# Sixteen more tokens of an expert layer go row by row (144 instead of 128), and the orders around them move with it

## The chip, the cores and the metric

The kernel runs on one core of one Trainium2 chip. The metric is the device time of one execution in microseconds (us). Within one execution times are counted from the start of the profiled span. The engines are TensorE (PE; PEld is its loading of weights), VectorE (DVE), ScalarE (ACT), GpSimd (POOL) and SyncE (SP), which issues most DMAs.

## What is computed

Two transformer blocks over 512 tokens of width 1024 in float32. The change concerns the last layer of the second, a mixture of 16384 one-neuron experts. Each of 8 heads picks 16 experts per token out of 128 x 128 by two top-16 searches; the 128 picked experts of a token have a gate `g_c` each:

```python
    def chunk(args):
        h_c, e_c, g_c = args
        a = jnp.einsum('cd,ced->ce', h_c.astype(jnp.float32), u[e_c].astype(jnp.float32))
        act = jax.nn.gelu(a, approximate=False) * g_c
        return jnp.einsum('ce,ced->cd', act, v[e_c].astype(jnp.float32))
```

`u` and `v` are 16384 x 1024 matrices; the result is added to the residual `x`.

## The kernel before

**Two ways for the tokens.** The first `ND` = 384 tokens go densely: all 16384 experts are computed for them with matmuls, and a gate matrix with zeros for the experts that were not picked selects. The last 128 tokens go row by row: for each of their 128 picks, GpSimd gathers one row of `u` per token (128 rows of 4 KB, one token per partition), VectorE multiplies it with the token's `h` and sums (a dot product); later the same with `v`, where VectorE adds the scaled row to `rows_o`. That makes 128 u jobs and 128 v jobs, in this order, each one gather (`gather`, L1697) and one VectorE pass (`one_by_one`).

**Dense u stage.** 128 blocks of 128 experts. A block's weights (512 KB) are loaded by SP, ScalarE rounds them to a high part `wh` (L85), VectorE subtracts to get the low part `wl` (helper line L217), and TensorE runs 24 matmuls of `ND` columns: 8 slices of the contraction times hi x hi, hi x lo, lo x hi (L429 to L431). Four raw weight buffers and three of parts are in flight. For the first `NPRE` = 60 blocks the low part was made during the feed-forward stage and stored in DRAM (`made`); GpSimd's queue fetches it (L108). ScalarE applies Gelu (L1880), and SP writes the block's activations to DRAM (`a_d`).

**Gates.** Within the u stage, after the top-16 searches (`select`, on VectorE), `gates` makes the dense gate matrix in batches of 8 tokens: VectorE builds one-hot matrices, ScalarE scales one (L1810), TensorE multiplies them (16 f16 matmuls a batch, L1770), and ScalarE evicts four tokens at a time from PSUM into a tile `stg` laid out expert by token (L1774). Each full tile of `NG` = 48 tokens is written to DRAM (`g_d`, `put`).

**Dense v stage.** The 128 blocks of v in their order: eight blocks of activations and gates are fetched from DRAM at a time (`fetch`, tile `ag`, which shares its two buffers with `stg`), VectorE multiplies them, ScalarE and VectorE split the product into high and low parts two blocks at a time (`activate`), and 24 matmuls of `ND` columns (L1939 to L1941) add to eight PSUM banks. At the end the rows are transposed into the remaining 128 columns of the banks, VectorE adds the residual (L1948), and the result is stored.

**What sets the order.** The program is one stream for every engine, written by a host-side loop. TensorE's matmuls are its clock: after each slice of a block (8 slices) `later.tick()` advances the waiting generators, which put the work of the other engines in between; `yield n` means n ticks. `Balance` keeps a rough count of TensorE, VectorE and DMA work: `room(slack)` lets a generator wait while VectorE is more than `slack` columns behind TensorE, and `fill` (called in each tick) starts a row job when VectorE and the DMA count have room, up to `RATE` jobs per u block, and in the v stage evenly up to block 124. `LAG` is the number of ticks between the two halves of a split. Row buffers: `NUB` = 4 of one kind (`ub`), which before hold the scores of two heads, scratch of `select` (`small`) and the norm weights (`grow`).

Of the kernel before, what the change touches and what calls it, by code (L numbers as in the profile page):

```python
# [236 lines left out]
def tile_kernel(ctx, tc, a, out):  # L237
# [61 lines left out]
    ents([("v", j) for j in range(128)])  # L299
# [1216 lines left out]
    stream.LAG = 4  # L1516
# [11 lines left out]
    def row_buffer():  # L1528
        return c3.tile([128, D], F32, name="ub", bufs=NUB)

    scs = [row_buffer().rearrange("p (i t) -> p i t", i=2) for h in HEADS[:2]]
# [52 lines left out]
    def together(gens):  # L1584
# [22 lines left out]
    def select(t0, nt, places):  # L1607
# [5 lines left out]
        for h in HEADS:  # L1613
            while not {2 * h, 2 * h + 1} <= ready3:
# [4 lines left out]
            yield from together(  # L1619
                top16(scs[h][:, i, 128 * t:128 * t + 128], v[:, i, t - t0, :], ix[:, i, t - t0, :])  # L1620
                for i in range(2) for t in range(t0, t0 + nt))
            dv.tensor_copy(ixf, ix)
            cand, ixr, oneh = places(nt)
            yield from room()
# [3 lines left out]
            for i in range(2):  # L1628
# [3 lines left out]
            yield from together(  # L1632
                top16(cand[:, t].rearrange("p a b -> p (a b)"), gf[:, t0 + t, h, :], si[:, t, :])
                for t in range(nt))
# [5 lines left out]
            yield from room()  # L1640
            dv.tensor_tensor(oneh, sab.rearrange("p i t k -> p (i t) k")[:, :, None, :].to_broadcast(
                [128, 2 * nt, 16, 16]), iota16[:, None].to_broadcast([128, 2 * nt, 16, 16]), op=OP.is_equal)
            yield from room()
            for i in range(2):
                part = oneh[:, nt * i:nt * i + nt]
                dv.tensor_tensor(part, part, ixr[i], op=OP.mult)
                yield from room()
            for n in (8, 4, 2):
                dv.tensor_tensor(oneh[:, :, :n], oneh[:, :, :n], oneh[:, :, n:2 * n], op=OP.add)
                yield from room()  # L1650
# [3 lines left out]
            yield from room()  # L1654
# [10 lines left out]
        yield from room()  # L1665
        dv.reciprocal(z, z)
        yield from room()
        dv.tensor_tensor(g, g, z[:, :, :, None].to_broadcast(full), op=OP.mult)
        yield from room()
# [17 lines left out]
    dots = c3.tile([128, 128], F32, name="dots")  # L1687
    rows_h = c3.tile([128, KD, 128], F32, name="rows_h")
    flat = {"u": a["u_rows"], "v": a["v"].rearrange("b p d -> (b p) d")}
    jobs = [(what, s) for what in "uv" for s in range(128)]  # L1690
    got, stage = {}, {"at": 0}

    def gather(n):
        if n < len(jobs):
            what, s = jobs[n]
            got[n] = row_buffer()
            nc.gpsimd.indirect_dma_start(out=got[n], out_offset=None, in_=flat[what],  # L1697
                                         in_offset=bass.IndirectOffsetOnAxis(ap=idx[:, s:s + 1], axis=0))
            bal.transfer(D)

    def rows_in():
# [3 lines left out]
        for i in range(2):  # L1705
            pt = pst.tile([128, 512], F32, name="pt")
            for k in range(4):
                nc.tensor.transpose(pt[:, 128 * k:128 * k + 128], xT[:, 4 * i + k, ND:], identf)
# [8 lines left out]
        while not {(t, HEADS[i]) for t in (0, ND // 128) for i in range(2)} <= read:  # L1717
            yield 1
        for n in range(NUB):
            gather(n)  # L1720
        yield 20
        stage["go"] = stage.get("blk", 0)

    def one_by_one():
        n = stage["at"]
        if "go" not in stage or n == len(jobs):
            return
        what, s = jobs[n]
        if what == "v" and "out" not in stage:
            return  # L1730
        t = got.pop(n).rearrange("p (k f) -> p k f", k=8)
        if what == "u":
            dv.tensor_tensor_reduce(t, t, rows_h, 1.0, 0.0, OP.mult, OP.add, dots[:, s:s + 1])
            if s == 127:
                nc.scalar.activation(dots, dots, AF.Gelu)
        elif s == 0:
            dv.tensor_tensor(dots, dots, gf[:, 3].rearrange("p h k -> p (h k)"), op=OP.mult)
            dv.tensor_scalar(stage["out"], t, dots[:, s:s + 1], None, op0=OP.mult)
# [17 lines left out]
    def gates():  # L1756
# [5 lines left out]
        prev = stg = None  # L1762

        def products(oh2, og, b):
            for q in range(TG // 4):
                pg = pss.tile([128, 512], F32, name="ps")
                for i in range(4):
                    for r in range(2):
# [4 lines left out]
                k0 = (TG * b + 4 * q) % NG  # L1773
                nc.scalar.activation(stg[:, :, k0:k0 + 4].rearrange("p e t -> p t e"),  # L1774
                                     pg.rearrange("p (t e) -> p t e", t=4), AF.Copy, scale=1.0 / GS)
                yield 1

        for b in range(ND // TG):
# [25 lines left out]
            yield from room()  # L1804
            dv.tensor_tensor(oh1, ib, of(eb[:, 0, tk]), op=OP.is_equal)
            yield from room()
            dv.tensor_tensor(og[:, 0], oh1, of(gp[:, tk]), op=OP.mult)
            yield from room()
# [5 lines left out]
            if prev:  # L1814
                yield from products(*prev)
                if TG * b % NG == 0:
                    later.spawn(put(TG * b // NG - 1, stg))
            if TG * b % NG == 0:
                stg = c3.tile([128, 128, NG], F32, name="stg", bufs=2)
            prev = oh2, og, b  # L1820
        yield from products(*prev)
        later.spawn(put(ND // NG - 1, stg))

    def put(i, stg):
# [14 lines left out]
    def fetch(c):  # L1839

        if c < 16:
            t = c3.tile([128, 2, 8, ND], F32, name="ag", tag="stg", bufs=2)
            for i in range(2):
                nc.sync.dma_start(t[:, 0, 4 * i:4 * i + 4].rearrange("p b t -> p (b t)"),
                                  a_d[2 * c + i].rearrange("p b t -> p (b t)"))
                bal.transfer(4 * ND)
                yield P["f1"]
            for i in range(2):
                nc.sync.dma_start(t[:, 1, 4 * i:4 * i + 4], g_d[4 * i:4 * i + 4, :, 8 * c:8 * c + 8, :].rearrange(
                    "s p b t -> p s (b t)"))  # L1850
# [223 lines left out]
```

## Time and profile before

| | |
|---|---|
| median of 3 runs | 2462.03 us (2460.21 to 2464.12) |
| the profiled execution | 2467.27 us, span 2463.4 us |
| granted TensorE clock, mean | 0.993 |
| TensorE matmuls, busy | 2384.7 us (97%) |
| VectorE, busy | 1797.7 us (73%) |
| ScalarE, busy | 1219.2 us (49%) |
| GpSimd, busy | 477.8 us (19%) |
| moved by DMA | 643.37 MB, mean 261 GB/s |

Busy time is the union of an engine's instructions; matmuls are pipelined and overlap, so a TensorE that is busy all the time need not run at its best. The granted clock is told as a share of full speed. The DMA share is the mean busy share of 16 DMA engines and can pass 1.

### The profile page before, as it was taken

To read this page: it belongs to the slowest core of one execution; us is meant where nothing else is said; L and a number is where in the kernel's file an instruction comes from. 1 tells how busy PE (TensorE), PEld (TensorE's weight loads), DVE (VectorE), ACT (ScalarE), POOL (GpSimd) and SP (SyncE) were. 2 spreads that over 40 slices of the span, in tenths; PEclk is the share of its full clock that TensorE was granted. 3 is DMA by queue.
4 is the path that set the end of the run, shared out by engine and by line. 5 is a ranking of instruction groups with operands and counts; after the bars stand their busy time and mean duration, and the time that the engine had idled before them with its cause. 6 is when DMAs were issued, how large, how long until landed. Compare 5 with 4: busy or idle time off the path is not lost.

```text
span 2463.4 us, 36419 instructions
## 1 busy us (share of the span) xinstructions
PE 2384.7 (97%) x13139; PEld 2134.6 (87%) x13139; DVE 1797.7 (73%) x3587; ACT 1219.2 (49%) x2185; POOL 477.8 (19%) x538
## 2 busy tenths in 40 slices
PE   6899999999999999999999999999999999999998
PEld 5677778888777888777889999999999999999998
DVE  6678676555676777655688997787766888888886
ACT  3466444443545555533445344999973333333332
POOL 0310001000012100000001233322113433334331
PEclk9999999999999999999999999999999999999999
DMA  7873679898856543134326999999989999999994
GB/s 277 204 205 103 226 236 315 282 292 280 265 156 176 150 126 110 58 107 145 105 85 231 321 407 406 364 322 328 330 323 395 378 373 368 358 370 366 374 376 154
DMA packets 210580, 643.37 MB, mean 261 GB/s; under 512 B 25488, under 2 KB 62096, under 8 KB 210016
## 3 DMA queue, kind: packets, MB, share of 16 engines
q1 hardware_dynamic: 141360, 412.46, 47.7%
q0 software_dynamic: 68320, 227.97, 28.0%
q8 instruction: 103, 1.69, 0.3%
q14 instruction: 77, 0.63, 0.1%
q10 hardware_dynamic: 720, 0.62, 0.1%
HBM read 540.92 MB, written 100.17 MB: 260 GB/s over the span
## 4 chain that ended last, share of the span: by engine, by line
PE 80%; ACT 7%; DVE 5%; issue 4%; DMA 4%; POOL 1%; ACTq 0%; SPq 0%; DVEq 0%; POOLq 0%
PE pg L429 17%; PE pg L431 16%; PE pg L430 16%; PE pv L1939 7%; PE pv L1941 7%; PE pv L1940 7%; ACT ogh L1810 2%; ACT stg L1774 2%; ACT wh L85 1%; PE pt L654 1%; PE po L676 1%; DMA wl<-made 1%; PE ps L780 1%; PE ps L1770 1%; DMA ks<-bounce 1%
## 5 line engine op out<-in xcount | busy, mean ns | idle before, releaser
L429 PE MATMUL pg<-hh,wh 128*128 128x512 f32 (+1 forms) x2088 | 789.4, 378 | 5.9 <-ACT c_rcnt L968 1.7
L431 PE MATMUL pg<-hh,wl 128*128 128x512 f32 (+1 forms) x2088 | 763.7, 366 | 4.7 <-DMA wl<-made 4.1
L430 PE MATMUL pg<-hl,wh 128*128 128x512 f32 (+1 forms) x2088 | 763.0, 365 | 2.2 <-DVE hl L500 1.1
L85 ACT ACTIVATE wh<-wr 128x1024 fp32r<-128x1024 f32 (+2 forms) x446 | 466.4, 1046 | 406.1 <-PE pv L1940 189.1
L431 PEld LDWEIGHTS pg<-hh,wl 128*128 128x128 f32 x2088 | 394.6, 189 | 52.0 <-DMA wl<-made 6.3
L429 PEld LDWEIGHTS pg<-hh,wh 128*128 128x128 f32 x2088 | 395.1, 189 | 44.7 <-ACT wh L85 2.1
L430 PEld LDWEIGHTS pg<-hl,wh 128*128 128x128 f32 x2088 | 396.0, 190 | 36.5 <-DVE hl L557 2.0
L217 DVE TENSOR_TENSOR wl<-wr,wh 128x1024 fp32r<-128x1024 f32 x210 | 256.9, 1223 | 139.1 <-ACT wh L85 138.3
L88 DVE TENSOR_TENSOR wl<-wr,wh 128x1024 fp32r<-128x1024 f32 (+2 forms) x176 | 209.4, 1191 | 45.6 <-ACT wh L85 45.6
L1697 POOL DMA_INDIRECT ub<-in_v,idx x128 | 163.4, 1276 | 293.4 <-DVE rows_o L217 275.3
L1697 POOL DMA_INDIRECT ub<-in_u_rows,idx x128 | 157.2, 1228 | 310.3 <-DVE dots L217 292.4
L1939 PE MATMUL pv<-part,wh 128*128 128x384 f32 x512 | 172.0, 336 | 0.6 <-ACT full L1880 0.6
L1941 PE MATMUL pv<-part,wl 128*128 128x384 f32 x512 | 172.1, 336 | 0.0
L1940 PE MATMUL pv<-part,wh 128*128 128x384 f32 x512 | 171.9, 336 | 0.0
L1939 PE MATMUL pv<-parts,wh 128*128 128x384 f32 x512 | 171.5, 335 | 0.0
L1940 PE MATMUL pv<-parts,wh 128*128 128x384 f32 x512 | 171.4, 335 | 0.0
L1941 PE MATMUL pv<-parts,wl 128*128 128x384 f32 x512 | 171.2, 334 | 0.0
L217 DVE CUSTOM_DVE_ANT_0 ub<-ub,rows_h 128x1024 f32<-128x1024 f32 x128 | 155.1, 1218 | 16.4 <-DMA ub<-in_u_rows,idx 14.5
L217 DVE SCALAR_TENSOR_TENSOR rows_o<-ub,dots,rows_o 128x1024 f32<-128x1024 f32 x127 | 162.6, 1280 | 0.8
L1810 ACT ACTIVATE ogh<-oh,gT 128x128 f16<-128x128 f16 x384 | 120.5, 457 | 2.3 <-DVE oh L217 2.3
L95 DVE TENSOR_TENSOR pl<-wr,ph 128x1024 fp32r<-128x1024 f32 x60 | 73.3, 1222 | 52.1 <-ACT ph L93 50.6
L1880 ACT ACTIVATE full<-pg 128x384 f32<-128x384 f32 x86 | 44.6, 519 | 125.8 <-issue 102.8
(409 smaller groups left out, 4018.3 us busy)
## 6 DMA issues: line engine op xcount, KB each, us to landing
wr<-in_u SPq DMA_DIRECT2D x188, 512.0 KB
wr<-in_v SPq DMA_DIRECT2D x128, 512.0 KB
wr<-in_w_in SPq DMA_DIRECT2D x66, 512.0 KB
made<-pl POOLq DMA_DIRECT2D x60, 512.0 KB
wl<-made POOLq DMA_DIRECT2D x60, 512.0 KB
g_d<-stg SPq DMA_DIRECT2D x32, 768.0 KB
ag<-a_d SPq DMA_DIRECT2D x32, 768.0 KB
ag<-g_d SPq DMA_DIRECT2D x32, 768.0 KB
```

Source lines behind the costliest of these rows:

```text
L85: self.nc.scalar.activation(hi[:, :n], t[:, :n], AF.Copy)
L88: self.low.tensor_tensor(lo[:, :n], t[:, :n], hi[:, :n].bitcast(F32), op=OP.subtract)
L95: self.low.tensor_tensor(lo, t, hi.bitcast(F32), op=OP.subtract)
L217: return f(*args, **kw)
L429: nc.tensor.matmul(ps[:m, :n], w[0][:, wk], rh, start=first, stop=False)
L430: nc.tensor.matmul(ps[:m, :n], w[0][:, wk], rl, start=False, stop=False)
L431: nc.tensor.matmul(ps[:m, :n], w[1][:, wk], rh, start=False, stop=last)
L1697: nc.gpsimd.indirect_dma_start(out=got[n], out_offset=None, in_=flat[what], in_offset=bass.IndirectOffsetOnAxis(ap=idx[:, s:s + 1], axis=0))
L1810: nc.scalar.activation(og[:, 1, n // 2, :, n % 2], oh1[:, n // 2, :, n % 2], AF.Copy, scale=gT[:, tk.start + n:tk.start + n + 1])
L1939: nc.tensor.matmul(ps, wh[:, c], hi, start=b == 0, stop=False)
L1940: nc.tensor.matmul(ps, wh[:, c], lo, start=False, stop=False)
L1941: nc.tensor.matmul(ps, wl[:, c], hi, start=False, stop=b == 127)
```

## The change

16 more tokens (368 to 383) go row by row: `ND` is 368, and a second kind of job is added. For them a gather takes 8 picks of 16 tokens at once (partition 16 g + t), so 128 picks need `NE` = 16 u jobs ("x") and 16 v jobs ("y"). Their `h` rows are copied to eight groups of partitions by seven small DMAs, indices and gates are spread by 24 small DMAs (`extra_in`), and at the end a matmul with `fold` (eight identity matrices on top of each other, 16 columns) sums the groups. Gate tiles hold `NG` = 46 tokens, and the eviction's inner loop runs over four tokens instead of 128 experts. The v stage begins with blocks 120 to 127, whose activations ScalarE writes straight into `ag`, without `a_d`. Row buffers are two of kind `ub` and two of kind `uc` (the scores of two heads): the first two gathers go out when the row tokens' search is done, the others in `deeper`. The diff, cut:

```diff
+ORDER_V = [*range(120, 128), *range(120)]
-ND = 384
-NG = 48
-NUB = 4
-NPRE = 60
-RATE = 0.95
+ND = 368
+NS = 384
+NE = NS - ND
+NG = ND // 8
+NPRE = 58
+RATE = 1.06
...
-    stream.LAG = 4
+    stream.LAG = 5
...
-    def row_buffer():
-        return c3.tile([128, D], F32, name="ub", bufs=NUB)
-
+    def row_buffer(tag="ub"):
+        return c3.tile([128, D], F32, name="ub", tag=tag, bufs=2)
+    scs = [row_buffer("uc").rearrange("p (i t) -> p i t", i=2) for h in HEADS[:2]]
...
-    jobs = [(what, s) for what in "uv" for s in range(128)]
+    jobs = [(what, s) for pair in ("ux", "vy") for what, n in zip(pair, (128, NE)) for s in range(n)]
...
+    def deeper():
+
+        while not {(0, h) for h in HEADS[:2]} <= read:
+            yield 1
+        stage["deep"] = stage["next"]
+        for n in range(2):
+            gather(stage["next"])
...
-        while not {(t, HEADS[i]) for t in (0, ND // 128) for i in range(2)} <= read:
+        for n in range(2):
+            gather(n)
+        later.spawn(deeper())
+        while "u" in busy:
             yield 1
-        for n in range(NUB):
-            gather(n)
-        yield 20
+        stage["rows_x"] = rows_x = cst.tile([128, KD, 128], F32, name="rows_x", tag="silc")
+        for i in range(2):
+            pt = pst.tile([128, 512], F32, name="pt")
+            for k in range(4):
+                nc.tensor.transpose(pt[:NE, 128 * k:128 * k + 128], xT[:, 4 * i + k, ND:NS], identf)
+            yield 3
+            dv.tensor_tensor(rows_x[:NE, 4 * i:4 * i + 4, :], pt[:NE].rearrange("p (k f) -> p k f", k=4),
+                             grow[:NE, 512 * i:512 * i + 512].rearrange("p (k f) -> p k f", k=4), op=OP.mult)
+            yield 1
+        for g in range(1, 128 // NE):
+            nc.sync.dma_start(rows_x[NE * g:NE * g + NE], rows_x[:NE])
+        yield 10
         stage["go"] = stage.get("blk", 0)
+
+    def extra_in():
+
+
+        dv.scalar_tensor_tensor(idx_t, e1f[:, 2].rearrange("p h k -> p (h k)"), 128.0,
+                                e2f[:, 2].rearrange("p h k -> p (h k)"), op0=OP.mult, op1=OP.add)
+        yield 4
+        t = slice(ND % 128, 128)
+        for g in range(128 // NE):
+            p, c = slice(NE * g, NE * g + NE), slice(NE * g, NE * g + NE)
+            nc.sync.dma_start(idx_x[p], idx_t[t, c])
+            nc.sync.dma_start(gf_x[p], gf[t, 2].rearrange("p h k -> p (h k)")[:, c])
+            nc.sync.dma_start(rt_x[p], rt[t, 0, 2:3])
+            yield 2
+        yield 10
+        stage["more"] = True
 
...
-        if "go" not in stage or n == len(jobs):
+        if "go" not in stage or n == len(jobs) or (stage["next"] >= 128 and "more" not in stage):
...
+        own = what in "uv"
+        d = dots if own else dots_x
+        if what in "ux":
+            dv.tensor_tensor_reduce(t, t, rows_h if own else stage["rows_x"], 1.0, 0.0, OP.mult, OP.add, d[:, s:s + 1])
+            if s == d.shape[1] - 1:
+                nc.scalar.activation(d, d, AF.Gelu, scale=1.0 if own else rt_x)
         else:
-            dv.scalar_tensor_tensor(stage["out"], t, dots[:, s:s + 1], stage["out"], op0=OP.mult, op1=OP.add)
-        gather(n + NUB)
+            o = stage["out"][:, 0 if own else 1]
+            if s == 0:
+                dv.tensor_tensor(d, d, gf[:, 3].rearrange("p h k -> p (h k)") if own else gf_x, op=OP.mult)
+                dv.tensor_scalar(o, t, d[:, s:s + 1], None, op0=OP.mult)
+            else:
+                dv.scalar_tensor_tensor(o, t, d[:, s:s + 1], o, op0=OP.mult, op1=OP.add)
+        gather(stage["next"])
...
-                k0 = (TG * b + 4 * q) % NG
-                nc.scalar.activation(stg[:, :, k0:k0 + 4].rearrange("p e t -> p t e"),
-                                     pg.rearrange("p (t e) -> p t e", t=4), AF.Copy, scale=1.0 / GS)
+                t0 = TG * b + 4 * q
+                for i in range(t0 // NG, (t0 + 3) // NG + 1):
+                    if i not in stg:
+                        stg[i] = c3.tile([128, 128, NG], F32, name="stg", bufs=2)
+                    lo, hi = max(t0, NG * i), min(t0 + 4, NG * i + NG)
+                    nc.scalar.activation(stg[i][:, :, lo - NG * i:hi - NG * i],
+                                         pg.rearrange("p (t e) -> p e t", t=4)[:, :, lo - t0:hi - t0], AF.Copy,
+                                         scale=1.0 / GS)
+                    if hi == NG * i + NG:
+                        later.spawn(put(i, stg.pop(i)))
...
-            yield from room()
+            yield from room(3500)
...
+        yield 10
         if i == ND // NG - 1:
-            yield P["f0"]
-            yield from fetch(0)
-            later.spawn(activate(0), 2)
+            while 15 not in AG:
+                yield 1
+            yield from fetch_g(15)
+            while stage["blk"] < 123:
+                yield 1
+            later.spawn(activate(0), 8)
             yield from fetch(1)
 
...
+    def fetch(i):
+
+        if i < 16:
+            c = ORDER_V[8 * i] // 8
+            yield from fetch_a(c)
+            yield from fetch_g(c)
...
+            if b >= 120:
+                nc.scalar.activation((AG[15] if b > 120 else eight(15))[:, 0, b % 8], ps, AF.Gelu)
+                return
...
-    later.spawn(chain(select(3, 1, places1), rows_in()))
-    later.spawn(chain(select(0, 3, places3), gates()))
+    later.spawn(chain(select(3, 1, places1, 4500), rows_in()))
+
+    def spread_out():
+        later.spawn(extra_in())
+        yield 0
+
+    later.spawn(chain(select(0, 3, places3, 2000), spread_out(), gates()))
...
-    rows_o = hp.tile([128, 4, KD, 128], F32, name="rows_o", tag="hh")[:, 0]
+    rows_o = hp.tile([128, 4, KD, 128], F32, name="rows_o", tag="hh")[:, :2]
-    for b in range(128):
-        stage["blk"] = b
...
+    for g in range(1, 128 // NE):
+        nc.vector.tensor_tensor(fold, identf[:, :NE] if g == 1 else fold, identf[:, NE * g:NE * g + NE], op=OP.add)
     for d in reversed(range(8)):
-        nc.tensor.transpose(acc_o[d][:, ND:], rows_o[:, d, :], identf)
+        nc.tensor.transpose(acc_o[d][:, NS:], rows_o[:, 0, d, :], identf)
+        nc.tensor.matmul(acc_o[d][:, ND:NS], rows_o[:, 1, d, :], fold, start=True, stop=True)
         nc.vector.tensor_tensor(xT[:, d, :], acc_o[d], xT[:, d, :], op=OP.add)
```

`places3`, `top16`, `together` and `select` change only in taking a `slack`; `together` and `select` hand it to `room`. The v blocks' weights are streamed in `ORDER_V` too.

## Rows read from the trace of the kernel before

**Rows 1.** Busy by stretch: us, PE, PEld, DVE, ACT, POOL, clock, DMA share, GB/s.

```profile
1321.50:1921.40 599.90, 590.34 (x3823) 569.93 (x3821) 466.02 (x1180) 404.41 (x802) 166.88 (x171) 0.99 0.96 352
1410.00:1550.00 140.00, 140.00 (x803) 138.28 (x802) 112.22 (x427) 61.13 (x103) 51.35 (x62) 1.00 1.06 405
1556.00:1824.00 268.00, 262.90 (x1953) 245.40 (x1952) 210.40 (x299) 263.16 (x569) 64.10 (x56) 0.99 0.92 327
1921.40:2425.00 503.60, 503.60 (x2902) 503.60 (x2903) 424.23 (x407) 173.52 (x183) 184.59 (x142) 1.00 0.97 366
1921.40:2455.00 533.60, 533.60 (x3076) 533.57 (x3077) 437.05 (x419) 180.29 (x190) 184.59 (x142) 1.00 0.93 347
2200.00:2250.00 50.00, 50.00 (x290) 50.00 (x289) 41.51 (x38) 17.15 (x18) 17.31 (x14) 1.00 0.95 348
```

**Rows 2.** TensorE in order of time: start us, duration us, instruction; first and last.

```profile
1212.56 0.27 PE L1573 MATMUL ps<-kl,hi 128*128 128x128 f32 x1
...
1213.34 0.27 PE L1574 MATMUL ps<-kh,lo 128*128 128x128 f32 x1
...
499.66 0.39 PE L431 MATMUL pg<-hh,wl 128*128 128x512 f32 x1
...
501.25 0.39 PE L429 MATMUL pg<-hh,wh 128*128 128x512 f32 x1
...
1999.77 0.33 PE L1940 MATMUL pv<-parts,wh 128*128 128x384 f32 x1
...
2001.33 0.33 PE L1940 MATMUL pv<-parts,wh 128*128 128x384 f32 x1
```

**Rows 3.** Groups by line, 1300 to 2464: count, busy us, mean ns, idle before.

```profile
L85 ACT ACTIVATE wh<-wr 128x1024 fp32r<-128x1024 f32 x256 | 271.7, 1062 | 339.9 <-PE pv L1940 189.1 <-issue 147.4 <-PE pv L1941 3.4
L217 DVE TENSOR_TENSOR wl<-wr,wh 128x1024 fp32r<-128x1024 f32 x196 | 239.9, 1224 | 138.9 <-ACT wh L85 138.0 <-issue 0.6
...
L1774 ACT ACTIVATE stg<-ps 128x512 f32<-128x512 f32 x96 | 98.2, 1135 | 0.1
...
L1565 ACT ACTIVATE hi<-pg 128x512 fp32r<-128x512 f32 x2 | 1.2, 598 | 3.5 <-PE pg L431 3.5
```

**Rows 4.** Line L1774: count, shortest, median, longest ns, first and last start.

```profile
L1774 ACT ACTIVATE stg<-ps x96: 1055/1136/1258, 1556.6 to 1823.3; 128x512 f32<-128x512 f32 x96
```

**Rows 5.** Groups by line of TensorE, 1560 to 1826.

```profile
L429 PE MATMUL pg<-hh,wh 128*128 128x384 f32 x391 | 140.3, 359 | 0.0
...
L1770 PE MATMUL ps<-ogh,oh2h 128*128 128x128 f16 x752 | 60.8, 221 | 4.7 <-ACT stg L1774 2.4 <-ACT ogh L1810 1.2
```

**Rows 6.** Row passes of VectorE: before 1921.4 (first row) and after.

```profile
L217 DVE CUSTOM_DVE_ANT_0 ub<-ub,rows_h 128x1024 f32<-128x1024 f32 x111 | 134.6, 1218 | 16.4 <-DMA ub<-in_u_rows,idx 14.5 <-issue 1.8
...
L217 DVE SCALAR_TENSOR_TENSOR rows_o<-ub,dots,rows_o 128x1024 f32<-128x1024 f32 x127 | 162.6, 1280 | 0.8
...
L217 DVE CUSTOM_DVE_ANT_0 ub<-ub,rows_h 128x1024 f32<-128x1024 f32 x18 | 21.7, 1220 | 0.7 <-DMA ub<-in_u_rows,idx 0.7
```

**Rows 7.** Waits of TensorE in the u stage: us in all, times, longest.

```profile
PE pg L431 <- DMA wl<-made: 4.1, 2, 3.8
PE ps L1770 <- ACT stg L1774: 2.4, 6, 0.7
PE ps L1770 <- ACT ogh L1810: 1.2, 1, 1.2
```

**Rows 8.** Short stretches: us, PE busy, granted clock, DMA share, GB/s.

```profile
1394.00:1396.00 2.00, 2.00 (x8) 0.50 0.72 284
...
1820.00:1822.00 2.00, 1.26 (x6) 0.50 0.85 268
```

**Rows 9.** The chain of waits around 1380: start us, us, what.

```profile
1380.83 10.60 DMA wl<-made
```

**Rows 10.** Waits of VectorE, 1885 to 1921: us in all, times, longest.

```profile
DVE ub L217 <- DMA ub<-in_u_rows,idx: 9.6, 10, 1.4
```

**Rows 11.** The end of the chain of waits.

```profile
2454.93 1.29 DVE xT L1948 x2
```

More of the change, by code (lines that the diff above doesn't have):

```diff
@@ L298, in tile_kernel @@
     ents([("u", j) for j in range(128)])
-    ents([("v", j) for j in range(128)])
+    ents([("v", j) for j in ORDER_V])
     xT = xp.tile([128, KD, S], F32, name="xT")
@@ L1590, in together @@
             for g in list(gens):
-                yield from room()
+                yield from room(slack)
                 if next(g, True):
@@ L1631, in select @@
             si = w3.tile([128, nt, 16], U32, name="si" + x)
-            yield from together(
+            yield from together((
                 top16(cand[:, t].rearrange("p a b -> p (a b)"), gf[:, t0 + t, h, :], si[:, t, :])
-                for t in range(nt))
+                for t in range(nt)), slack)
             sa = w3.tile([128, 2, nt, 16], U32, name="sa" + x, bufs=1)
@@ L1653, in select @@
                                  op=OP.add)
-            yield from room()
+            yield from room(slack)
             read.add((t0, h))
@@ L1695, in gather @@
             what, s = jobs[n]
-            got[n] = row_buffer()
-            nc.gpsimd.indirect_dma_start(out=got[n], out_offset=None, in_=flat[what],
-                                         in_offset=bass.IndirectOffsetOnAxis(ap=idx[:, s:s + 1], axis=0))
-            bal.transfer(D)
+            more = stage.get("deep", len(jobs))
+            got[n] = row_buffer("uc" if n >= more and (n - more) % 4 < 2 else "ub")
+            stage["next"] = n + 1
+            nc.gpsimd.indirect_dma_start(out=got[n], out_offset=None, in_=flat["u" if what in "ux" else "v"],
+                                         in_offset=bass.IndirectOffsetOnAxis(
+                                             ap=(idx if what in "uv" else idx_x)[:, s:s + 1], axis=0))
+            bal.transfer(D)
+    def deeper():
[4 more added lines that the diff above has]
+            gather(stage["next"])
     def rows_in():
@@ L1724, in one_by_one @@
     def one_by_one():
         n = stage["at"]
-        if "go" not in stage or n == len(jobs):
+        if "go" not in stage or n == len(jobs) or (stage["next"] >= 128 and "more" not in stage):
             return
         what, s = jobs[n]
-        if what == "v" and "out" not in stage:
+        if what in "vy" and "out" not in stage:
             return
         t = got.pop(n).rearrange("p (k f) -> p k f", k=8)
[L1732 to L1738, printed above, removed]
-        else:
-            dv.scalar_tensor_tensor(stage["out"], t, dots[:, s:s + 1], stage["out"], op0=OP.mult, op1=OP.add)
@@ L1925, in tile_kernel @@
     acc_o = [psv.tile([128, 512], F32, name="pv%d" % d) for d in range(8)]
[L1926 removed]
+    rows_o = hp.tile([128, 4, KD, 128], F32, name="rows_o", tag="hh")[:, :2]
     stage.update(out=rows_o, blk=0)
[L1928 to L1933 removed]
+    for i, b in enumerate(ORDER_V):
+        stage["blk"] = i
+        if i % 8 == 5:
+            later.spawn(fetch(i // 8 + 2))
+        if i % 2 == 0:
+            later.spawn(activate(i + 2))
         wh, wl = stream.get(("v", b))
```

89 lines of the change are left out of this document (44 added, 45 removed).

## The prediction

> **What bounds the kernel now.** I read the busy time by stretches first, then the spacing of matmuls on TensorE, then the groups of instructions by line, then the waits. The u stage (128 blocks of u, 1321.5 to 1921.4) lasts 599.9 us and the v stage (128 blocks of v, to 2455) 533.6 us; together they are 46% of the span, and only they change by more than a few instructions. In the v stage TensorE is busy for all of its 533.6 us; in the u stage for 590 of 600 [rows 1]. The reader is to see that TensorE alone sets the pace there: VectorE is busy for 437 of 534 us and for 466 of 600.
>
> A busy engine of pipelined matmuls could still be waiting, so I take starts. Successive matmuls start 0.1733 us apart with 384 columns (nine gaps, 1999.77 to 2001.33), 0.2271 us with 512 columns (seven gaps, 499.66 to 501.25) and 0.111 us with 128 columns (seven gaps, 1212.56 to 1213.34) [rows 2]. [...] A block is 24 matmuls, 4.16 us.
>
> One stretch is different. While the gate matrices are made (1556 to 1824), ScalarE is busy for 263 of 268 us and TensorE shows idle time [rows 1], with waits on the eviction (2.4 us) and on `ogh` (1.2 us) [rows 7]; 48 batches of 8 tokens take 1823.3 - 1556.6 = 266.7 us, 5.6 us each [rows 4]. TensorE's own need there is 1173 matmuls x 0.1733 = 203 us plus 752 gate matmuls [rows 5], so ScalarE and TensorE are close to balance, ScalarE a little behind.
>
> The DMA engines are the other near limit: 366 GB/s in the v stage until the fetching ends, 405 GB/s over 140 us early in the u stage, and TensorE was busy for all of those 140 us [rows 1].
>
> **The change, step by step.** *Fewer columns.* 384 becomes 368 in 128 x 24 = 3072 matmuls of u and as many of v. By the slope, 16 columns x 0.42 = 6.7 ns each: 20.6 us in each stage, 41.2 us in all. By bare proportion (0.1733 x 16/384 = 7.2 ns) it would be 44 us; I take 41.2, since the slope is what two widths show.
>
> *Fewer gate batches.* 46 instead of 48, so 32 matmuls fewer. They cost at most (266 - 203)/752 = 83 ns each [rows 5], at least the 53 ns of 128 columns at 0.42 ns: 1.7 to 2.7 us, taken as 2.
>
> *The eviction L1774.* Now it reads 512 contiguous values and writes each 192 bytes from the last: 1135 ns, against 598 ns for a plain 512-column eviction [rows 3]. The change writes four tokens contiguously and reads every 128th value of PSUM. No row shows such a read. Below, 0.60 us (the scattered write was the whole excess); above, 1.135 + 0.537 = 1.67 us (the read costs as much, and the write gains nothing). I take about 0.7: the write was what was scattered, and a run of four is three quarters contiguous. Then 92 evictions save about 40 us of ScalarE, it falls out of the bound, and the few us that TensorE loses to it come back. What is lost in that stretch now: 3.6 us of waits [rows 7] and matmuls at a granted clock of 0.50, the lower level, after the idle time around 1820 [rows 8]. I count 3 us of gain, between 0 and 9. Four groups of four tokens straddle two `stg` tiles, which adds four evictions, hidden.
>
> *32 more gathered rows.* 16 u and 16 v jobs, each 512 KB, one GpSimd issue and one VectorE pass of 1.22 or 1.28 us [rows 6]: 40 us on VectorE, 16.8 MB. The reader who adds 40 to the time would be wrong as long as VectorE has idle time: 134 us in the u stage, 97 in the v stage [rows 1]. Now some 110 rows are done before the v stage and 146 inside it [rows 6]. `RATE` 1.06 with a start some five blocks earlier allows 1.06 x 120 = 127 before v; the scheduler's own DMA budget holds it to less while `made` is read, so I take 124, which leaves 164 in v, 18 more. VectorE in v: 437 + 18 x 1.28 - 5 (activation pairs 4% narrower) = 455 of 513 us, 89%. Without that cover each row would cost its 1.28 us.
>
> *DMA in v.* 347 GB/s x 533.6 us = 185 MB now [rows 1]; 9.4 MB more for 18 rows, 1.8 less for narrower chunks: 193 MB, to be fetched in 513 us less some 10 us at the end (estimate), so 384 GB/s. That lies between 366, what v does now, and 405, what the chip held for 140 us. At 405 nothing shows; at 366 the stage takes 193/366 + 10 = 537 us, 24 too many. I take 6, nearer the row that was sustained with TensorE full. Late gathers make VectorE wait: from 1885 to 1921, with rows 2.4 us apart, it waited 9.6 us in ten waits [rows 10] and TensorE lost nothing; in v they will be 3.0 us apart. [...]
>
> *The start.* Four gathers issued together from 1376 on delayed the landing of a `made` low part to 10.6 us [rows 9]; TensorE waited 3.8 us [rows 7] and ran at the lower clock level (0.50) after it [rows 8]. Now two go first, two later. But the second takes the buffer of `grow`, which the product for `rows_x` still reads: GpSimd's queue stands there for about eight ticks (one block, 4 us), and the `made` fetches queue behind it, with two blocks (8 us) of lead. So 2 us of gain, between +6 (all of the stall gone) and -4 (another one like it).
>
> *Costs of nothing.* On SP 31 small DMAs join (7 for `rows_x`, 24 for the spread indices); they wait on VectorE at most for its allowed backlog of some 2 us, and behind them stand weight loads with four raw buffers (16 us) of lead. `NPRE` 58: two subtractions of 1.22 us and two conversions leave the feed-forward stage and two subtractions join u, all on engines with idle time; 1 MB less is read. `LAG` 5 and the slacks shift VectorE by at most 2 us against low parts made two blocks ahead. Blocks 120 to 127 skipping DRAM removes 8 writes and one 1.5 MB fetch, cover for DMA alone; the gates must be finished by block 120 for it, and they end near block 105. Eight rows_x transposes, and after the last matmul one small product per output tile under the 0.65 us VectorE add [rows 11]: 1 us in all.
>
> Sum: -20.6 - 20.6 - 2 - 3 + 6 - 2 + 1 = -41.2. The profiled execution took 2467.3 us, 5.2 above the median of the runs; I take the difference off the median: 2462 - 41 = 2421.
>
> **Rivals.** *Eviction unchanged* (0.17). ScalarE keeps the gate stretch: 46 batches x 5.5 = 253 us for 47 blocks and two more at 4.0 us, 261 instead of 267. Of the 13 us counted there (49 blocks x 0.16, gates, waits) 6 remain: 2428. If the looser room (3500) packs 1.2 batches per block, ScalarE needs about 5.2 us for each (a sixth of a block's 1.06 us split [rows 3] and of its Gelu less), 239 us for 38 blocks and 11 x 4.0 after it: 283, so 2450. For it: no row shows the read; against: the plain eviction's 598 ns. [...]
>
> *DMA becomes the bound of v* (0.14; the other side). At 366 GB/s 2421 + 18 = 2439; at 348, the rate of the chunk-heavy 50 us stretches [rows 1], 193/348 + 10 = 565 us, 46 over the 519 counted: 2467, slower. It decides from about 350 GB/s down. For it: v already takes 366 of what may be its ceiling; against it are the 405 GB/s. [...]
>
> *Matmuls don't shorten* (0.02): weight loads are shown busy for all of the v stage [rows 1]; were they the pace, only the small terms would remain, 2460. The 0.111 us spacing speaks against it.
>
> *Something else is late* (0.07): gates not done by block 120, or rows left over after v at 1.28 us each; 32 of them would take back the gain. 15 blocks of margin and 11% of VectorE speak against it.
>
> **How the numbers follow.** The forecast holds 0.60 with its own range 2402 to 2432: all good bounds together give -20.6 - 20.6 - 2.7 - 9 - 6 = -59, 2403; the bad ones within it (6 us of start, 12 of DMA) about 2432. To hold 8 in 10 the range reaches through the eviction case and the mild DMA case: 2402 to 2452. A measurement of this kernel can tell about 0.2%, 5 us. Slower than 2467: 0.05 of the DMA case, 0.05 of the last, 0.01 of the eviction at its upper bound (0.11); within 5 us: the weight case, 0.02 of the last and 0.01 of DMA (0.05); the rest, 0.84, is faster.
>
> **What the profile after would show.** Matmuls of v 0.1667 us apart, v stage about 513 to 520 us; u stage about 570 to 575; L1774's successor below 0.8 us and ScalarE no longer full from 1556 on; about 164 rows in v, VectorE near 89% there, DMA near 385 GB/s with no TensorE wait on `wh` or `wl`. Wrong would be: v longer than 525 us with waits on DMA or `wl`; an eviction above 1.1 us; rows after the last matmul of v.

## The result and the profile after

The changed kernel takes 2422.9 us (median of 4 runs, 2417.93 to 2424.62) against 2462.8 for the kernel before in the same session: ratio 0.9832, 95% interval 0.9819 to 0.9844. The forecast was 2421 (2402 to 2452). The total came out; several terms of its sum did not, as the experiments show. The profiled execution spans 2420.9 us.

Busy time by stretches of the changed kernel (columns as in [rows 1]): the u stage, its start, the start of the gates, and the v stage.

```profile
1309.40:1896.60 587.20, 573.13 (x3846) 554.46 (x3844) 481.57 (x1188) 363.41 (x795) 198.16 (x186) 0.99 0.99 366
1350.00:1400.00 50.00, 42.18 (x239) 40.97 (x238) 41.29 (x176) 17.88 (x32) 14.05 (x18) 0.97 1.07 368
1550.00:1600.00 50.00, 47.96 (x317) 46.51 (x316) 42.71 (x64) 29.30 (x66) 24.47 (x19) 0.97 0.93 340
...
1896.60:2412.00 515.40, 515.37 (x3076) 515.33 (x3077) 450.01 (x440) 179.57 (x191) 257.83 (x158) 1.00 0.95 372
```

TensorE still fills the v stage, now 515.4 us instead of 533.6; VectorE has 450 of 515 (87%) and the engines move 372 GB/s, 366 x 587 + 372 x 515 = 407 MB in both stages. The u stage takes 587.2 us instead of 608.8, both counted from its first matmul (1312.6 in the kernel before). Its start got worse: TensorE is idle for 7.8 of the 50 us from 1350 on, where the kernel before has 3.8.

Matmuls of v in order of time (start, duration, instruction), the first and last of 121 in 20 us, so 20.11/120 = 0.1676 us apart; the answer to [rows 2].

```profile
2099.77 0.33 PE L2018 MATMUL pv<-parts,wl 128*128 128x368 f32 x1
...
2119.88 0.33 PE L2018 MATMUL pv<-parts,wl 128*128 128x368 f32 x1
```

The eviction (L1774 before, L1829 now; shortest, median and longest ns, first and last start), the answer to [rows 4]:

```profile
L1829 ACT ACTIVATE stg<-ps x96: 376/602/645, 1554.8 to 1837.5; 128x512 f32<-128x512 f32 x88, 128x256 f32<-128x256 f32 x8
```

602 ns instead of 1136: reading every 128th value of PSUM costs ScalarE next to nothing beside a plain 512-column eviction (598 ns, [rows 3]).

TensorE's waits from 1300 to 2425 (times, longest), the answer to [rows 7]:

```profile
PE pg L433 <- DMA wl<-made: 8.7, 5, 2.6
PE pg L431 <- ACT au L1952: 2.4, 2, 2.0
PE pg L431 <- DVE lo L219: 1.0, 1, 1.0
PE pv L2016 <- ACT ag L1949: 0.6, 1, 0.6
PE ps L1821 <- ACT stg L1829: 0.5, 1, 0.5
```

The waits on the eviction are gone (0.5 us instead of 2.4), those on early-made low parts have doubled (8.7 instead of 4.1). (`au`, like `full` further down, is a tile that Gelu writes.) GpSimd in order of time shows why:

```profile
1340.72 1.05 POOL L1707 DMA_INDIRECT ub<-in_u_rows,idx  x1 [2.99 <-DVE og L219]
1345.21 1.01 POOL L1707 DMA_INDIRECT ub<-in_u_rows,idx  x1 [3.44 <-DVE sa L219]
1346.22 1.17 POOL L110 DMA_DIRECT2D wl<-made  x2
...
1358.18 1.01 POOL L1707 DMA_INDIRECT ub<-in_u_rows,idx  x1 [0.31 <-DVE ti L219]
1359.50 0.99 POOL L1707 DMA_INDIRECT ub<-in_u_rows,idx  x1 [0.30 <-issue]
1361.36 0.56 POOL L110 DMA_DIRECT2D wl<-made  x1 [0.87 <-PE pg L433]
1368.25 1.45 POOL L1707 DMA_INDIRECT ub<-in_u_rows,idx  x1 [6.33 <-DVE dots L219]
1369.68 0.62 POOL L110 DMA_DIRECT2D wl<-made  x1
...
1381.85 1.01 POOL L1707 DMA_INDIRECT ub<-in_u_rows,idx  x1 [0.30 <-issue]
1383.16 0.99 POOL L1707 DMA_INDIRECT ub<-in_u_rows,idx  x1 [0.30 <-issue]
1384.98 0.56 POOL L110 DMA_DIRECT2D wl<-made  x1 [0.83 <-PE pg L433]
```

TensorE's waits on such fetches up to 1400:

```profile
1353.12 0.43 PE L433 MATMUL pg<-hh,wl 128*128 128x368 f32 x1 [2.56 <-DMA wl<-made]
...
1371.01 0.43 PE L433 MATMUL pg<-hh,wl 128*128 128x368 f32 x1 [1.61 <-DMA wl<-made]
...
1376.75 0.43 PE L433 MATMUL pg<-hh,wl 128*128 128x368 f32 x1 [1.49 <-DMA wl<-made]
...
1395.16 0.43 PE L433 MATMUL pg<-hh,wl 128*128 128x368 f32 x1 [2.15 <-DMA wl<-made]
```

A low part is due about every 4 us, so each fetch can be matched with the block that uses it. Two of the waits are for fetches that left late. The second gather stands 3.44 us for the buffer of `grow`, two fetches leave together behind it at 1346.22, and TensorE waits for the first of them until 1353.12. At 1368.25 a gather has stood 6.33 us for a row pass that itself waited for a gather in flight; the fetch behind it leaves at 1369.68 instead of about 1365, and TensorE waits for it until 1376.75. The other two are for fetches that left in time, at 1361.36 and 1384.98, but right behind two gathers: TensorE could use them only 9.65 and 10.18 us after they left, where two blocks of lead are about 8. That these landings are slow because of the gathers is read from the order of time alone.

The row passes of VectorE that fall in v, from the groups by line (answer to [rows 6]):

```profile
L219 DVE SCALAR_TENSOR_TENSOR rows_o<-ub,dots,rows_o 128x1024 f32<-128x1024 f32 x127 | 162.7, 1281 | 7.0 <-DMA ub<-in_v,idx 5.8
...
L219 DVE CUSTOM_DVE_ANT_0 ub<-ub,rows_x 128x1024 f32<-128x1024 f32 x16 | 19.2, 1219 | 1.5 <-DMA ub<-in_u_rows,idx_x 1.5
L219 DVE SCALAR_TENSOR_TENSOR rows_o<-ub,dots_x,rows_o 128x1024 f32<-128x1024 f32 x15 | 19.2, 1280 | 0.4 <-DMA ub<-in_v,idx_x 0.3
...
L219 DVE CUSTOM_DVE_ANT_0 ub<-ub,rows_h 128x1024 f32<-128x1024 f32 x2 | 2.4, 1223 | 0.2 <-DMA ub<-in_u_rows,idx 0.2
```

With the two first v passes (one of each kind) they are 162, and they waited 8 us for gathers while TensorE lost nothing.

### The profile page after: what moved, and what is told of

Same layout as the page of the kernel before. It is cut to its first block, busy times and chain, and to the rows that moved or that the text cites. A ratio compares the mean times of both kernels' runs of the same rounds, so it can differ in the third digit from the quotient of the medians.

```text
span 2420.9 us, 36478 instructions
## 1 busy us (share of the span) xinstructions
PE 2342.7 (97%) x13131; PEld 2096.7 (87%) x13131; DVE 1824.1 (75%) x3640; ACT 1171.1 (48%) x2168; POOL 581.0 (24%) x566
## 4 chain that ended last, share of the span: by engine, by line
PE 83%; DMA 7%; DVE 5%; issue 2%; ACT 2%; SPq 1%; POOL 1%; ACTq 0%; DVEq 0%; POOLq 0%
PE pg L431 18%; PE pg L433 17%; PE pg L432 17%; PE pv L2017 7%; PE pv L2018 7%; PE pv L2016 7%; DMA ub<-in_u_rows,idx 2%; PE pt L656 1%; DMA wl<-made 1%; PE ps L1821 1%; PE po L678 1%; PE ps L782 1%; PE po L582 1%; DMA ks<-bounce 1%; DMA a_d<-au 1%
## 5 line engine op out<-in xcount | busy, mean ns | idle before, releaser
L433 PEld LDWEIGHTS pg<-hh,wl 128*128 128x128 f32 x2088 | 394.2, 189 | 58.5 <-DMA wl<-made 10.9
L1707 POOL DMA_INDIRECT ub<-in_v,idx x128 | 209.4, 1636 | 185.7 <-DVE rows_o L219 160.6
L1707 POOL DMA_INDIRECT ub<-in_u_rows,idx x128 | 164.5, 1285 | 248.0 <-DVE dots L219 216.7
L2016 PE MATMUL pv<-part,wh 128*128 128x368 f32 x512 | 169.3, 331 | 0.6 <-ACT ag L1949 0.6
L2017 PE MATMUL pv<-parts,wh 128*128 128x368 f32 x512 | 169.8, 332 | 0.0
L2017 PE MATMUL pv<-part,wh 128*128 128x368 f32 x512 | 169.5, 331 | 0.0
L2018 PE MATMUL pv<-parts,wl 128*128 128x368 f32 x512 | 169.3, 331 | 0.0
L2018 PE MATMUL pv<-part,wl 128*128 128x368 f32 x512 | 168.8, 330 | 0.0
L2016 PE MATMUL pv<-parts,wh 128*128 128x368 f32 x512 | 168.0, 328 | 0.0
L1868 ACT ACTIVATE ogh<-oh,gT 128x128 f16<-128x128 f16 x368 | 114.7, 438 | 8.9 <-issue 4.8
L99 POOL DMA_DIRECT2D made<-pl x58 | 30.8, 532 | 297.4 <-DVE pl L97 297.4
```

Source lines behind the costliest of these rows:

```text
L433: nc.tensor.matmul(ps[:m, :n], w[1][:, wk], rh, start=False, stop=last)
L1868: nc.scalar.activation(og[:, 1, n // 2, :, n % 2], oh1[:, n // 2, :, n % 2], AF.Copy, scale=gT[:, tk.start + n:tk.start + n + 1])
L2016: nc.tensor.matmul(ps, wh[:, c], hi, start=i == 0, stop=False)
L2017: nc.tensor.matmul(ps, wh[:, c], lo, start=False, stop=False)
L2018: nc.tensor.matmul(ps, wl[:, c], hi, start=False, stop=i == 127)
```

## The experiments

Every kernel was timed beside the kernel before, on the same chip. Stages are read from the first matmul of u, the first of v and the first final add, in the profiled execution.

| kernel | us, median | ratio, 95% | u stage | v stage |
|---|---|---|---|---|
| before | 2462.8 to 2465.0 | 1 | 608.8 | 533.5 |
| after | 2422.9 | 0.9832 (0.9819–0.9844) | 587.3 | 515.5 |
| e_evict_old | 2438.4 | 0.9895 (0.9879–0.9912) | 605.2 | 515.6 |
| e_before_evict | 2453.0 | 0.9954 (0.9942–0.9966) | 599.3 | 533.5 |
| e_nd376 | 2455.0 | 0.9965 (0.9952–0.9978) | 608.4 | 527.3 |
| e_nd352 | 2480.1 | 1.0064 (1.0049–1.0080) | 627.4 | 533.9 (37.1 of it a wait) |
| e_norows | 2421.3 | 0.9826 (0.9812–0.9840) | 586.7 | 515.5 |
| e_vdma | 2438.3 | 0.9890 (0.9875–0.9906) | 589.4 | 533.7 |
| e_orderv | 2430.0 | 0.9868 (0.9851–0.9885) | 588.2 | 518.5 |
| e_npre60 | 2416.5 | 0.9807 (0.9793–0.9820) | 578.5 | 515.5 |
| e_start | 2412.9 | 0.9789 (0.9776–0.9803) | 575.7 | 515.6 |
| e_combo | 2412.2 | 0.9787 (0.9774–0.9800) | 576.2 | 515.5 |
| e_repl | 2419.3 | 0.9811 (0.9798–0.9825) | 582.5 | 515.6 |
| e_best | 2410.7 | 0.9785 (0.9771–0.9798) | 575.0 | 515.6 |

**The eviction, undone.** e_evict_old:

```diff
-                    nc.scalar.activation(stg[i][:, :, lo - NG * i:hi - NG * i],
-                                         pg.rearrange("p (t e) -> p e t", t=4)[:, :, lo - t0:hi - t0], AF.Copy,
+                    nc.scalar.activation(stg[i][:, :, lo - NG * i:hi - NG * i].rearrange("p e t -> p t e"),
+                                         pg.rearrange("p (t e) -> p t e", t=4)[:, lo - t0:hi - t0], AF.Copy,
```

> The changed kernel with only the eviction put back: it reads 512 contiguous values and writes each one four tokens apart, as in the kernel before. My theory: the eviction goes from 609 ns back to about 1135 ns, ScalarE gets 88 x 0.53 = 46 us more work in the gate stretch, of which most lies in idle time (ScalarE is busy for 73 of 100 us from 1600 to 1700), so the time rises by 1 to 8 us, to 2424 to 2431 us. The rival that the eviction decides the stretch, as worked out ahead: 2428 to 2450, the upper end if the gates are then finished only after the last eight blocks need them.

It cost 15.5 us, twice the most that I expected, and inside the rival's span. The eviction's line, TensorE's waits, and the stretch 1700 to 1840 of this kernel:

```profile
L1829 ACT ACTIVATE stg<-ps x96: 627/1123/1240, 1549.5 to 1851.1; 128x512 f32<-128x512 f32 x88, 128x256 f32<-128x256 f32 x8
```
```profile
PE ps L1821 <- ACT stg L1829: 13.2, 23, 1.7
```
```profile
1700.00:1840.00 140.00, 131.22 (x1012) 122.54 (x1011) 107.68 (x155) 139.13 (x308) 31.48 (x25) 1.00 0.92 327
```

ScalarE is full (139 of 140) and TensorE loses 13.2 us in 23 waits on it over the u stage.

**The eviction alone.** e_before_evict, on the kernel before:

```diff
-                nc.scalar.activation(stg[:, :, k0:k0 + 4].rearrange("p e t -> p t e"),
-                                     pg.rearrange("p (t e) -> p t e", t=4), AF.Copy, scale=1.0 / GS)
+                nc.scalar.activation(stg[:, :, k0:k0 + 4],
+                                     pg.rearrange("p (t e) -> p e t", t=4), AF.Copy, scale=1.0 / GS)
```

> The kernel before (384 columns, 128 tokens by rows, all else as it was) with only the eviction changed to four tokens innermost. My forecast counted this part at 3 us, between 0 and 9, in a stretch where only 3.6 us of TensorE waits and some time at the lower clock level were to be had: 2454 to 2463 us. Rival: it is worth as much here as in the changed kernel, where putting the old order back cost 15.5 us: 2445 to 2450.

It gained 0.46% (0.34 to 0.58), 11 us (8 to 14): more than the 3 forecast, at the edge of its bounds, and less than the rival's 15. The stretch 1556 to 1824 of this kernel, to be laid beside the same stretch in [rows 1]:

```profile
1556.00:1824.00 268.00, 267.98 (x2009) 252.80 (x2007) 211.07 (x300) 231.50 (x574) 84.80 (x58) 1.00 0.93 338
```

TensorE does 2009 matmuls there instead of 1953, and the 56 more are all of 384 columns: 56 x 0.173 = 9.7 us, the 9.5 by which the u stage is shorter. Idle time before was only 5.1 of 268 us, waits 3.6. Some 2 us more went to the granted clock of 0.50 at the end of the stretch (after 1819 [rows 8]; with the eviction changed it stays at 1.00); the rest of the loss had stood inside the busy time of pipelined matmuls. Counting matmuls per stretch shows it; counting waits doesn't.

**Columns.** e_nd376 (`ND = 376`) and e_nd352 (`ND = 352`, `RATE = 1.15`), all else as changed.

> Half of the step in columns: 376 columns and 136 tokens by rows. TensorE theory: matmuls 0.1706 us apart, half way from 0.1677 to 0.1735 (if the 5.85 ns are one price per column), 2 x 3072 x 2.9 ns = 18 us more than 368: 2437 to 2444. Rival (a step instead of a slope, the width 384 being odd in some way): the spacing stays at 0.1677 or goes to 0.1735, and the time to about 2423 or 2455.

> The same change once more in the same direction: 352 columns, 160 tokens by rows (32 more gathered rows), RATE 1.15. If TensorE stays the bound and each of 2 x 3072 matmuls saves another 5.85 ns, the time is 2422 - 36 = 2386 us, 2384 to 2392. If the DMA engines have a ceiling of about 405 GB/s, the v stage needs 193 + 9.4 - 1.8 + some = 203 to 208 MB, 501 to 513 us and some 10 at the end, instead of 497: 2400 to 2412 us, with TensorE waits on DMA in v. [...] The spacing itself is a third point for the price of a column: 0.1617 us if 5.85 ns for 16 columns hold, 0.1609 if 0.42 ns per column hold from here.

First and last matmul starts of 118 (376 columns) and of 127 (352 columns) in 20 us of v:

```profile
2099.80 0.33 PE L2016 MATMUL pv<-part,wh 128*128 128x376 f32 x1
...
2119.84 0.34 PE L2016 MATMUL pv<-part,wh 128*128 128x376 f32 x1
```
```profile
2099.74 0.32 PE L2016 MATMUL pv<-part,wh 128*128 128x352 f32 x1
...
2119.96 0.32 PE L2016 MATMUL pv<-parts,wh 128*128 128x352 f32 x1
```

So 0.1734 (20.12/116 in the same 20 us of the kernel before), 0.1713, 0.1676 and 0.1605 us at 384, 376, 368 and 352 columns: the first 8 columns off save 2.1 ns, the next 8 3.7, the next 16 7.1. The price isn't one slope. From 512 to 384 and from 384 to 352 it is 0.42 and 0.41 ns per column; 368 lies 0.7 ns and 376 1.2 ns above that line. Why was not tried.

Neither width beat 368. At 376 v is 11.8 us longer than at 368 (3072 x 3.8 ns), but u is 21 longer: beside another 11.8 for columns stand 7.7 us of TensorE waiting on ScalarE, whose Gelu waited for its buffer to be written out. The time equals the rival's 2455, but not for the rival's reason: the spacing is near the theory's 0.1706. ScalarE's waits, 1540 to 1600:

```profile
ACT full L1952 <- DMA a_d<-full: 14.2, 2, 10.4
```

At 352 the matmuls got their price and the time went up. TensorE's waits:

```profile
PE pv L2027 <- DVE fold L2024: 37.1, 1, 37.1
PE ps L1821 <- ACT stg L1829: 30.3, 7, 12.0
PE pv L2016 <- ACT part L1940: 20.2, 1, 20.2
PE pg L433 <- DMA wl<-made: 10.5, 8, 4.4
```

I had expected waits on DMA in v; there were none. The gates ran to 1916, the last block of u; from block 120 on the activations of the last eight blocks take one of the two `stg` buffers, so the gate matrices waited for the one buffer left to be written out (the eviction for `g_d<-stg`, 15.4 us the longest). The granted clock was 0.81 from 1840 to 1900 and 0.79 from 1900 to 2000. And row passes were left over after the last matmul of v (`fold`, 37.1 us). That is the rival called "something else is late", both halves of it. 178 passes fell in v instead of 162. Why the rows fell behind is argued only: 32 more of them are 16.8 MB against 407 MB in stages that already move 366 and 372 GB/s.

**Rows taken away.** e_norows leaves the 32 extra passes out:

```diff
-    jobs = [(what, s) for pair in ("ux", "vy") for what, n in zip(pair, (128, NE)) for s in range(n)]
+    jobs = [(what, s) for pair in ("ux", "vy") for what, n in zip(pair, (128, 0)) for s in range(n)]
...
```

> The changed kernel without the 32 gathered rows of the sixteen extra tokens (the output of those tokens is left out; the widths stay at 368). If the rows are hidden under TensorE, as the forecast had it, only the waits near the start of u and the DMA load change: 2417 to 2423 us. If they cost what the reader would add up who counts VectorE or DMA time as time, 32 x 1.25 = 40 us go: 2383.

The ratio's interval overlaps that of the changed kernel, and v is 515.5 us in both. 1900 to 2300 without the rows, and with them (changed kernel):

```profile
1900.00:2300.00 400.00, 400.00 (x2389) 400.00 (x2388) 328.26 (x303) 140.68 (x149) 147.50 (x104) 1.00 0.96 361
```
```profile
1900.00:2300.00 400.00, 400.00 (x2388) 400.00 (x2387) 356.32 (x346) 141.66 (x150) 210.71 (x130) 1.00 1.00 393
```

28 us more of VectorE and 32 GB/s more, and TensorE does the same work.

**Bytes added in v.** e_vdma:

```diff
+        if 8 <= i < 124:
+            q = i % 4
+            nc.sync.dma_start(rows_h[:, 2 * q:2 * q + 2, :], a["v"][i, :, :256].rearrange("p (k f) -> p k f", k=2))
```

> The changed kernel with 128 KB more to fetch in each of 116 blocks of v (15.2 MB, into the dead rows_h, used by nothing). If the DMA engines have a ceiling near the 405 GB/s seen, the v stage must fetch 191.7 + 15.2 = 207 MB, 511 us at 405 and some 10 at the end, where TensorE needs 515: 2426 to 2436 us, with waits on weights. [...] If there is room above 420 GB/s: 2422 to 2425, and the windows of v show 420 GB/s.

v grows by 18.2 us. The stretch 1900 to 2400 and TensorE's waits from 1900 on, with the bytes added:

```profile
1900.00:2400.00 500.00, 489.10 (x2876) 483.82 (x2875) 426.11 (x412) 171.37 (x182) 236.16 (x156) 1.00 1.03 404
```
```profile
PE pv L2021 <- DVE wl L219: 6.3, 9, 0.7
PE pv L2020 <- DVE parts L219: 3.1, 7, 0.5
PE pv L2019 <- ACT parts L1940: 1.4, 1, 1.4
```

In none of its 50 us stretches did it move more than 410 GB/s, with a share of 1.01 to 1.03. The time is 2 us past the span expected for a ceiling near the 405 GB/s that u had shown [rows 1]; the changed kernel moves 393 from 1900 to 2300. The added loads also stand in SP's queue ahead of weight loads; what that costs by itself was not tried.

**The order of v undone.** e_orderv:

```diff
-ORDER_V = [*range(120, 128), *range(120)]
+ORDER_V = [*range(128)]
...
-            if b >= 120:
-                nc.scalar.activation((AG[15] if b > 120 else eight(15))[:, 0, b % 8], ps, AF.Gelu)
-                return
```

> The changed kernel with the v blocks in their plain order, 0 to 127, and all of u's activations written to DRAM and read back, as before; the rest as changed. My forecast gave this part no time of its own (8 writes of 188 KB and one fetch of 1.5 MB, hidden): 2421 to 2427 us. Rival: near the ceiling of the DMA engines the 3 MB more show in v or at the end of u: 3.0 MB at 407 GB/s is 7.4 us, 2428 to 2432.

The rival's 7 us came (9 by the ratios): ratio 0.9868 (0.9851 to 0.9885), an interval that does not meet that of the changed kernel. ScalarE in order of time, at the end of u in this kernel:

```profile
1889.21 0.48 ACT L1945 ACTIVATE full<-pg 128x368 f32<-128x368 f32 x1 [3.51 <-DMA a_d<-full]
...
1897.54 0.48 ACT L1945 ACTIVATE full<-pg 128x368 f32<-128x368 f32 x1 [6.90 <-DMA a_d<-full]
```

The last Gelus stand for their buffers to be written to DRAM through loaded DMA engines (378 GB/s at a share of 0.97 from 1840 to 1880), and the first matmul of v waits 5.9 us for such a Gelu. Staying on the chip removes that wait (0.6 us in the changed kernel). Another 3 us are in v, most of them from 1898 to 1903, right after the wait, where matmuls start 0.31 us apart instead of 0.17. The u stage of this profiled execution is only 0.9 us longer all the same, since its first 120 blocks took 5.6 us less than those of the changed kernel, which this edit does not explain.

**The start of u.** e_npre60 is `NPRE = 60`; e_start holds the row passes:

```diff
             nc.sync.dma_start(rows_x[NE * g:NE * g + NE], rows_x[:NE])
-        yield 10
+        while "deep" not in stage:
+            yield 1
+        yield 24
```

e_combo is both. e_repl adds ScalarE copies of the sixteen columns in place of the seven DMAs. e_best is e_combo with the second gather after the products:

```diff
-        for n in range(2):
-            gather(n)
-        later.spawn(deeper())
+        gather(0)
...
+        gather(1)
+        later.spawn(deeper())
```

> The changed kernel with the number of low parts made early put back from 58 to 60. If those two low parts are what made everything ahead of the u stage 3.2 us shorter, the first matmul of u comes some 3 us later and the time is 2424 to 2427 us. If the 3.2 us have another cause (the order of the instructions of the rows, or noise between executions), the time stays at 2423 within 1 us.

> The changed kernel, but the row passes start only once all four row gathers have been issued and 24 ticks (three blocks) have gone by, so that no pass, and no GpSimd gather behind a pass, waits for a gather that is still in flight. My theory: the wait of GpSimd for VectorE (6.3 us) goes, the low parts fetched behind it come in time, most of the 7.8 us that TensorE waits between 1340 and 1400 goes: 2415 to 2419 us. Rival: the waits come from the load of the DMA engines by the gathers and the copies of rows_x themselves, not from the queue of GpSimd; then the time stays at 2422 to 2425.

> The changed kernel with both of the edits that made it faster by themselves: 60 low parts made early (2416.5 alone) and the row passes held until four gathers are out and 24 ticks have passed (2412.9 alone). Theory: they lift different losses (60 low parts the waits around 1575, the held rows those around 1371 to 1395), so a good part of both adds: 2405 to 2411 us. Rival: both only lift the same waits of the start of u; then 2411 to 2416.

> The same two edits, and the eight copies of the sixteen extra tokens' rows are made by copying their columns eight times on ScalarE ahead of the transposes; the seven small DMAs on SP are gone. Theory: the TensorE wait at 1353 (2.6 us, a low part that lands late while the DMA engines are at a share of 1.25 in 1350 to 1360) comes from those DMAs, it was there in all runs with them (1.5 to 2.8 us), and goes: 1 to 4 us less than the two edits alone. Rival: it comes from the gathers; then the time stays within 1 us of the two edits alone.

> 60 low parts made early, row passes held, and the second row gather issued only after the products for rows_x, so that GpSimd no longer stands 3.4 us at the buffer of grow with two low parts queued behind it. In the two kernels that hold the row passes the low part due at about 1341 to 1344 went out at 1349 (3.4 us of standing, then a TensorE wait of 1.3 or 2.8 us); where the product came later still (the columns copied on ScalarE) GpSimd stood 5.3 us and TensorE waited 4.2. Theory: with the queue free the wait at about 1355 goes, 1 to 3 us: 2409 to 2411 us. Rival: the DMA engines' load at 1350 to 1360 is the cause, whatever the queue does: 2412 within 1.

Holding the passes brought 10 us: the waits of 1371 to 1395 (5.3 us in three) are down to one of 0.5, and the lower clock after them is gone (1.00 from 1350 to 1400). Only 6 us of it stand by block 40 of u. The rest comes while the gates are made, where the waits on `au` and a second stretch at the lower clock are gone too; what links them to the row passes was not tried. 60 low parts went the other way than expected: 6 us faster, not slower (ratio intervals 0.9793 to 0.9820 and 0.9819 to 0.9844, which just meet), with its first matmul of u at 1309.8 (1309.4 in the changed kernel). So `NPRE` didn't make the 3.2 us ahead of u; that matmul came between 1307.7 and 1313.1 in all fourteen kernels. Both edits together gave no more than the one, so they lift largely the same losses; with 60 low parts the waits for low parts and for `au` are 6.8 and 1.3 us instead of 8.7 and 2.4, and the granted clock stays at 1.00 where the changed kernel shows 0.50 (1396 to 1398) and 0.73 (1576 to 1578). Why two low parts do that is not settled.

The copies' theory fell. In e_repl the products came later, GpSimd stood longer, and TensorE's wait grew to 4.17 us. GpSimd and TensorE in e_repl:

```profile
1348.61 1.04 POOL L1707 DMA_INDIRECT ub<-in_u_rows,idx  x1 [5.33 <-DVE rows_x L219]
1349.65 1.18 POOL L110 DMA_DIRECT2D wl<-made  x2
```
```profile
1357.11 0.46 PE L433 MATMUL pg<-hh,wl 128*128 128x368 f32 x1 [4.17 <-DMA wl<-made]
```

In e_best a low part leaves between the two gathers, and TensorE is busy for all of 1340 to 1365:

```profile
1343.52 1.05 POOL L1707 DMA_INDIRECT ub<-in_u_rows,idx  x1 [3.00 <-DVE og L219]
1344.57 0.64 POOL L110 DMA_DIRECT2D wl<-made  x1
1348.02 1.03 POOL L1707 DMA_INDIRECT ub<-in_u_rows,idx  x1 [2.82 <-DVE sa L219]
```

The queue is the cause of that wait, the one at 1353 in the changed kernel. A wait of 1.16 us is left at 1382.66, for a fetch that left in time behind two gathers. In time, e_best can't be told from e_combo; it is ahead of the changed kernel by 0.5%, and of the kernel before by 2.15% (2.02 to 2.29).

## Why the prediction was right, and where it was not

By stages the forecast was -27.6 us in u (columns, gates, eviction, start), -14.6 in v (columns, DMA) and +1 for small things. The two profiled executions differ by -3.2 ahead of the first matmul of u, -21.5 in u, -18.0 in v and +0.3 at the end. (The 570 to 575 us that the forecast names for u are counted from 1321.5; on that count u took 578.) Nothing in the forecast stands for the 3.2; u gained 6 less than forecast and v 3 more. That these meet in the total is luck.

- *What bounds it*: right. TensorE set v except where bytes were added (e_vdma) and at the end of e_nd352, and rows were free (e_norows); 162 of them fell in v, with 164 forecast.
- *Columns*, -20.6 in each stage: right in mechanism, mis-sized. v became 18.0 us shorter. The slope, (0.2271 - 0.1733)/128 = 0.42 ns per column, was taken between 384 and 512; 368 lies 0.7 ns above its line.
- *Eviction*, -3: right in mechanism and in the operation's price (0.7 us counted, 0.60 measured), mis-sized in what it is worth: 11 us alone, 15.5 undone. The step that failed read TensorE's loss from its waits and the time at the lower clock.
- *DMA in v*, +6: 0. The value chosen between 0 at 405 GB/s and 24 at 366 should have been the lower bound: 193 MB were counted, 372 GB/s x 515 us = 192 MB were moved, and e_vdma moved 404 GB/s over 500 us. The rival was near all the same: 15.2 MB more brought 2438 us, where the rival had 2439.
- *The start*, -2: wrong in sign. The stand of GpSimd for `grow` came as described (3.44 us for "about four"), but two blocks of lead did not cover it; row passes waiting for gathers held the queue again, which no step named; and two gathers at a time still delayed two fetches to 9.65 and 10.18 us, as four had delayed one before (10.6 [rows 9]). TensorE's waits on low parts went from 4.1 to 8.7 us, where the forecast had them shrink. Holding the passes gives 10 us back.
- *Costs of nothing*: the order of v is worth 7 us, since 8 writes through engines at a share of 0.97 were not cover alone but stood ahead of the first matmul of v. Taking two early low parts away wasn't free either (6 us, e_npre60), cause open.
- *Gates and the last 1 us* weren't measured by themselves. The gates ended at 1838, in block 113 of the 120 that they had, later than the forecast's block 105. The eviction is not the reason: with it put back they end in block 113 as well, and changed alone, in block 105 as before. With the row passes held they end in block 109.

The parts overlap and don't add: -36 for columns (18 measured in v, as much assumed in u), -11 to -15 for the eviction, -7 for the order, +10 for the start (against held passes, not against the kernel before) and +6 for two low parts, of which the last two share most, and -2 for gates. The total was met because two errors one way, too much gain counted for columns and no loss for the start, stood against three the other way, a DMA loss that did not come and too little gain for the eviction and the order.

## What to carry to other kernels

Where an engine is nearly full, count the instructions that the bounding engine finishes in the stretch: its waits may show less than half of its loss (here 3.6 of 9.5 us). A gather that waits for a buffer holds what is queued behind it (here 3.44 us, with two fetches behind it); start consumers only when their gathers have landed, and put the fetch with a due time ahead. Match each fetch with the instruction that waits for it: a wait next to a late fetch can belong to an earlier one that left in time. Before a kernel is pushed further the same way, try a smaller and a larger step: here both were slower, 376 columns mostly by its matmuls, 352 by waits that 368 did not show.

## What the runs showed of the hardware

- ScalarE read PSUM with a stride of 128 values and wrote runs of four in 0.58 to 0.60 us for 512 columns; runs of one, 192 or 184 bytes apart, took 1.12 to 1.14 us (medians).
- With bytes added the core moved 404 GB/s from 1900 to 2400 (at most 410 in 50 us), and TensorE waited 10.9 us; at 393 (1900 to 2300 of the changed kernel) it did not wait, nor in a 50 us stretch at 405 (2250 to 2300 of the same kernel).
- The spacing of matmuls is not linear in columns: 0.2271, 0.1734 and 0.1605 us at 512, 384 and 352 lie on one line, 0.1713 at 376 and 0.1676 at 368 lie 1.2 and 0.7 ns above it.
